# Background loads a tile ahead, background pieces between products, and the first up weights fetched during the output projection, in a fused retention, Fourier and convolutional FFN layer

## The chip, the core and the metric

The kernel runs as one program on one core of a Trainium2 chip. The metric is the device time of the whole program in microseconds. The five engines have in-order queues of their own: TensorE (PE) multiplies, VectorE (DVE), ScalarE (ACT) and GpSimd (POOL) compute elementwise, and SyncE (SP) issues most DMA transfers from one queue. Engines wait for each other by semaphores.

## What is computed

One layer of a diffusion backbone on 2048 tokens of width 1024, in float32. The part ahead of the change is a token mixer (retention heads and Fourier groups), followed by the parts that the change touches: the output projection with its norm and residual, and a gated convolutional FFN.

```python
x = x + gt_a * rms_norm(mix, g_mix_post)          # mix = concat(retention, fourier) @ w_out
h = modulate(rms_norm(x, g_ffn_pre), sh_f, sc_f)
u = conv3_along_rows(h @ w_up) + conv_b           # 1024 -> 2*2816, three taps within rows of 64 tokens
a, b = split(u)
x = x + gt_f * rms_norm((silu(a) * b) @ w_down, g_ffn_post)
```

## The kernel before

Tokens lie along the free axis, in four blocks `b` of 512; channels lie on the 128 partitions, in tiles `n` of 128 channels. Each float32 operand is split into a rounded half and a rest (`split`: ACT writes `hi`, DVE subtracts to get `lo`), and each product is made of three matmuls (`mm3`).

The stages follow one another on PE: context and value product; four retention heads; the Fourier part; the output projection; up pass 0 (token blocks 0 and 1); down pass 0; up pass 1 (blocks 2 and 3); down pass 1; a tail. The weights of the FFN are multiplied by a Strassen-like scheme with seven products instead of eight; the sums of weight blocks that it needs are made on the chip. Sums of the down weights (`wsum`) are made in `w_sums` while the retention heads run and are kept in device memory.

*Output projection.* `mix_mm` makes 32 products, block by block. Its square sums `accm` are reduced to one row by a matmul with ones (`mix_cols`: a `pc` product, then `rp` on DVE, then a power on POOL into `rcm`). `mix_rows` spreads the row over the partitions: for blocks 0 and 1 by a product (`pb`), for blocks 2 and 3 by a trip through device memory (`row_m`, `rr_m`). `mix_post` then scales a tile by the norm and the gate, adds the residual `xt`, stores the tile (`x`), and adds its squares to `accx`, which the second norm needs (`x2_cols`, `x2_rows`, `rr_n`). The list `steps` says after which product each of these pieces is written. Blocks 2 and 3 are left to `rest_of_mix`, a generator that runs in the background of up pass 0; their tiles (`mt`) come back from device memory.

*Up passes.* `up_pass` runs over weight tiles `j`. Those in `ones_` are single products; the others are pairs of seven products of 12 matmuls each (84 in a pair). `operands` loads the weights (`ur`, or in pass 1 stored sums `us`) and splits them into `u_a...` and `u_s...`, LEAD = 6 ahead of PE. In a pair the products `a`, `b`, `c`, `d` go to PSUM banks; `psf` (an add on DVE, line 1368) has to read bank `a` before the pair's seventh product, which `last_of_pair` writes in the middle of the next pair, can add to it. `conv` and `gate` (tiles `y`) follow on ACT, DVE and POOL, and stores of `y` go out by SP. After each pair, `run_some(bg, nbg)` runs `nbg` pieces of the background generators: 2 in pass 0, 3 (GN) in pass 1.

*Background of pass 1.* `Norm.squares` sums squares of the down product of pass 0, and `Norm.finish(True)` ends each of its two token blocks: column sums (`pc`, `rp`, `rcf`), a trip of the row through device memory (`row_f`, `rr_f`), then for each of eight tiles a load of the tile (`ft`) and of the residual (`xf`), a product and an add (on DVE for odd tiles, on POOL for even ones), and a store to `out`.

The order of the instructions on the engines is set by a list scheduler: each instruction has its place in the program as priority, and goes ahead of earlier ones whenever it is ready by the scheduler's own clock. `tc.high_priority` moves a stretch forward in that priority. So the place of a piece in the program is not its place in a queue.

Of the kernel before, what the change touches and what calls it, by code (L numbers as in the profile page):

```python
# [9 lines left out]
F32 = mybir.dt.float32  # L10
# [18 lines left out]
LATE_S = {"s1": "s3", "a12": "s4"}  # L29
# [11 lines left out]
FW = 2, 1, 3  # L41
# [8 lines left out]
SENG = {"s1": "vector", "s2": "vector", "s3": "vector", "s4": "vector"}  # L50
# [7 lines left out]
def kern(tc, A, out):  # L58
    nc = tc.nc

    with ExitStack() as es:
# [140 lines left out]
        def w_sums():  # L202

            for k in range(KH):
                for c in (slice(0, 256), slice(256, TB)):
                    w = sump.tile([P, 4, 256], F32, tag="sum", name="wsum")
                    for i in range(2):
                        nc.sync.dma_start(w[:, 2 * i:2 * i + 2], A["w_down"][k + KH * i].rearrange("p (n c) -> p n c", n=2)[:, :, c])
                    yield
                    for o, l, r, op in ((3, 1, 3, ALU.add), (1, 0, 1, ALU.subtract), (0, 3, 0, ALU.subtract), (2, 2, 0, ALU.subtract)):  # L210
                        nc.vector.tensor_tensor(w[:, o], w[:, l], w[:, r], op=op)
                        yield
                    nc.sync.dma_start(wds[k][:, :, c], w)
# [460 lines left out]
        ws = w_sums()  # L674
        units = []
# [89 lines left out]
        for part in range(2):  # L765
# [56 lines left out]
            for lt in range(4):  # L822
                p1, p3 = zprod(2 * part, lt), zprod(2 * part + 1, lt)
# [94 lines left out]
        tp, txt, trr, trm = tg(po_, "pt", 5), tg(po_, "xt", 3), tg(po_, "rr", 1), tg(po_, "rrm", 1)  # L918
# [16 lines left out]
        accm, accx, rcm, rrm, rrn, r2d = {}, {}, {}, {}, {}, {}  # L935

        def mix_post(b, n):
            if n == 0:
                accx[b] = po_.tile([P, TB], F32, tag="acc", name="accx", bufs=2)
# [6 lines left out]
            nc.sync.dma_start(xt, A["xT"][n, :, b * TB:(b + 1) * TB])  # L946
            nc.vector.scalar_tensor_tensor(m, m, G1[:, n:n + 1], rrm[b], ALU.mult, ALU.mult)
            nc.vector.tensor_tensor(m, m, xt, op=ALU.add)
            nc.sync.dma_start(x2scr[n][b], m)
            sq_add(tp, accx[b], m, n == 0)  # L950
# [42 lines left out]
        def mix_cols(b):  # L993
            rcm[b] = cst([P, 4], f"rcm{b}", po_)
            sum_cols(accm[b], rcm[b], 4, po_)

        def mix_rows(b):
            if b < 2:
                rrm[b] = bcast_row(trm, rcm[b], 4, f"m{b}")
            else:  # L1000
                rrm[b] = row_in(trm, row_out(rcm[b], 4, f"m{b}"), 4, f"m{b}")
# [111 lines left out]
        steps = {}  # L1113

        def at(t, f, *a):
            steps.setdefault(t, []).append((f, a))
        for b in range(NB - 1):
            for k in range(4):
                at(RS[0] * b + RS[1] * k // 2, load_r, b + 1, k)
        for b in range(NB):  # L1120
            at(8 * b + 9, mix_cols, b)
        at(10, mix_rows, 0)
        at(19, mix_rows, 1)
        T = {}
        tf = t_first(T, 0)
        for n in range(KT):
            at(11 + n, mix_post, 0, n)
            at(19 + n, mix_post, 1, n)
            at(24 + n, next, tf)
        at(20, x2_cols, 0)  # L1130
        at(22, x2_rows, 0)
        at(28, x2_cols, 1)
        for t in range(SEEDS):
            seed_mix(t)
        for t in range(32):
            mix_mm(t // KT, t % KT)
            for f, a in steps.get(t, ()):
                f(*a)


        def rest_of_mix():
            mix_cols(3)
            for b in (2, 3):
                mix_rows(b)
                yield
                for n in range(KT):
                    mix_post(b, n)
                    yield
# [610 lines left out]
```

## Time and profile before

| | |
|---|---|
| runs | 2265.41, 2267.44, 2261.84 us; median 2265.41 |
| profiled execution | 2262.55 us, of which the span is 2260.8 |
| granted TensorE clock, mean | 0.966 |
| PE busy | 2095.5 us, 93% of the span |
| DVE busy | 1608.3 us, 71% |
| ACT, POOL busy | 1009.6 us (45%), 678.4 us (30%) |
| data moved | 395.20 MB, 175 GB/s over the span |
| PE idle, released by `psf` on DVE | 57.0 us |
| PE idle, released by `u_a` on ACT | 16.5 us |

The stages in the profiled execution, in us from the start: context and value product to 190, heads to 600, Fourier part to 690, output projection to 837, up pass 0 to 1320, down pass 0 to 1541 (its end overlaps the first operands of up pass 1), up pass 1 to 2010, down pass 1 and tail to 2260.8. Busy time counts matmuls with modelled ends, so a stage in which PE is busy for all of its length has no gap, while a stage with gaps shows them as length less busy time. Idle time is put down to the engine whose semaphore ended it.

### The profile page before, as it was taken

Reading aid. Unit: us, or ns where it says so; the run is one execution under the profiler, and the core shown is the slowest. Engines: PE = TensorE matmul, PEld = TensorE weight load, DVE = VectorE, ACT = ScalarE, POOL = GpSimd, SP = SyncE. Lnnn points to the kernel's source line nnn. Section 1 sums busy time; section 2 is a strip of 40 time slices with the busy share of each in tenths; the row PEclk is TensorE's granted clock in tenths of the full one; section 3 lists DMA queues with packets and bytes.
Section 4 is the critical chain, followed back from the end, with each engine's and each line's share of the span. In section 5 each row is a group of like instructions: output and inputs, shape, how many; then the busy total and the mean of one; then the engine's idle time right before and its main releaser. Section 6 shows DMA issues by size and latency. Waiting matters only on the chain.

```text
span 2260.8 us, 28205 instructions
## 1 busy us (share of the span) xinstructions
PE 2095.5 (93%) x9819; PEld 1725.6 (76%) x9819; DVE 1608.3 (71%) x2301; ACT 1009.6 (45%) x1754; POOL 678.4 (30%) x541
## 2 busy tenths in 40 slices
PE   7999899999999977899999999998899799999996
PEld 3777778887888755678778888886678678888886
DVE  6887786767565469987888777778576566675557
ACT  4443233334444555445454544545345345553441
POOL 4102222222110553333433341133233322331016
PEclk9999999999999988999999999999999999999997
DMA  8676633325451363655645578655463554376553
GB/s 305 222 231 214 199 126 109 90 79 140 142 215 52 112 174 136 192 192 144 189 174 155 172 274 284 232 192 195 138 207 127 167 185 135 131 262 227 190 168 112
DMA packets 202590, 395.20 MB, mean 175 GB/s; under 512 B 31816, under 2 KB 69584, under 8 KB 202448
## 3 DMA queue, kind: packets, MB, share of 16 engines
q1 hardware_dynamic: 194416, 367.07, 50.1%
q0 software_dynamic: 7600, 26.23, 3.2%
q8 instruction: 77, 1.26, 0.2%
q14 instruction: 65, 0.53, 0.1%
q10 hardware_dynamic: 432, 0.11, 0.0%
HBM read 275.33 MB, written 118.00 MB: 174 GB/s over the span
## 4 chain that ended last, share of the span: by engine, by line
PE 37%; DVE 5%; DMA 4%; issue 2%; ACT 1%; POOL 1%; SPq 0%; DVEq 0%; ACTq 0%; POOLq 0%
PE psu L92 7%; PE psu L94 7%; PE psu L93 7%; PE psd L92 5%; PE psd L94 5%; PE psd L93 5%; DMA row_f<-rcf 1%; DMA xf<-x 1%; DVE y L1218 1%; DMA draw<-fb 0%; DMA ft<-fo 0%; DMA draw<-in_w_down 0%; DVE y L1219 0%; DVE u_a L85 0%; ACT y L1215 0%
## 5 line engine op out<-in xcount | busy, mean ns | idle before, releaser
L85 DVE TENSOR_TENSOR dlo<-draw,dhi 128x1024 fp32r<-128x1024 f32 x154 | 203.7, 1346 | 115.5 <-ACT dhi L84 101.7
L1259 POOL TENSOR_TENSOR y<-y,y 128x512 f32<-128x512 f32 x82 | 124.0, 1512 | 475.5 <-DVE y L1219 329.8
L93 PE MATMUL psd<-dlo,dhi 128*128 128x512 f32 (+1 forms) x660 | 248.7, 378 | 2.4 <-DVE dlo L85 2.4
L94 PE MATMUL psd<-dhi,dlo 128*128 128x512 f32 (+1 forms) x660 | 247.6, 377 | 0.0
L84 ACT CAST dhi<-draw 128x1024 fp32r<-128x1024 f32 x154 | 159.7, 1051 | 163.0 <-PE psd L94 112.7
L92 PE MATMUL psd<-dhi 128*128 128x512 f32 (+1 forms) x660 | 211.2, 378 | 0.6 <-DVE cx L1520 0.6
L92 PE MATMUL psu<-t,u_s 128*128 128x512 f32 x492 | 199.3, 405 | 7.3 <-ACT t L84 5.7
L93 PE MATMUL psu<-t,u_s 128*128 128x512 f32 x492 | 198.3, 403 | 4.5 <-DVE t L85 4.5
L94 PE MATMUL psu<-t,u_s 128*128 128x512 f32 x492 | 197.5, 401 | 0.0
L92 PE MATMUL psu<-b,u_a 128*128 128x512 f32 x424 | 168.2, 397 | 16.5 <-ACT u_a L84 16.5
L94 PE MATMUL psu<-b,u_a 128*128 128x512 f32 x424 | 166.9, 394 | 0.0
L93 PE MATMUL psu<-b,u_a 128*128 128x512 f32 x424 | 166.9, 394 | 0.0
L1215 ACT ACTIVATE y<-psu,cb,cw 128x512 f32<-128x512 f32 x135 | 104.6, 776 | 101.7 <-PE psu L94 74.8
L85 DVE TENSOR_TENSOR u_a<-ur,u_a 128x512 fp32r<-128x512 f32 x147 | 130.3, 890 | 23.5 <-ACT u_a L84 23.4
L93 PEld LDWEIGHTS psd<-dlo,dhi 128*128 128x128 f32 x660 | 126.0, 191 | 25.2 <-DVE dlo L85 2.8
L92 PEld LDWEIGHTS psd<-dhi 128*128 128x128 f32 x660 | 125.2, 191 | 23.3 <-DVE cx L1520 0.8
L94 PEld LDWEIGHTS psd<-dhi,dlo 128*128 128x128 f32 x660 | 125.9, 191 | 22.2
L1218 DVE SCALAR_TENSOR_TENSOR y<-psu,cw,y 128x504 f32<-128x504 f32 x135 | 99.5, 738 | 53.9 <-ACT y L1215 53.9
L85 DVE TENSOR_TENSOR u_s<-us,u_s 128x512 fp32r<-128x512 f32 x103 | 91.9, 893 | 46.7 <-ACT u_s L84 46.7
L92 PE MATMUL psu<-t,u_a 128*128 128x512 f32 x164 | 67.6, 412 | 57.0 <-DVE psf L1368 57.0
L92 PEld LDWEIGHTS psu<-t,u_s 128*128 128x128 f32 x492 | 97.0, 197 | 29.1 <-ACT t L84 7.3
L93 PEld LDWEIGHTS psu<-t,u_s 128*128 128x128 f32 x492 | 96.6, 196 | 27.6 <-DVE t L85 6.9
(435 smaller groups left out, 5393.7 us busy)
## 6 DMA issues: line engine op xcount, KB each, us to landing
ur<-in_w_up SPq DMA_DIRECT2D x74, 512.0 KB, 5.5
draw<-wd SPq DMA_DIRECT2D x88, 256.0 KB, 5.9
draw<-ft SPq DMA_DIRECT2D x88, 256.0 KB, 5.7
ft<-y SPq DMA_DIRECT2D x36, 512.0 KB, 6.1
draw<-in_w_down SPq DMA_DIRECT2D x66, 256.0 KB, 5.3
draw<-fb SPq DMA_DIRECT2D x66, 256.0 KB, 5.6
xt<-in_xT SPq DMA_DIRECT2D x56, 256.0 KB, 4.6
adaw<-in_wadaB SPq DMA_DIRECT2D x24, 512.0 KB, 6.5
```

Source lines behind the costliest of these rows:

```text
L84: nc.scalar.copy(hi, src)
L85: nc.vector.tensor_tensor(lo, src, hi.bitcast(F32), op=ALU.subtract)
L92: nc.tensor.matmul(ps, lhi, rhi, start=start, stop=False, skip_group_check=on)
L93: nc.tensor.matmul(ps, lhi, rlo, start=False, stop=False, skip_group_check=on)
L94: nc.tensor.matmul(ps, llo, rhi, start=False, stop=stop, skip_group_check=on)
L1215: nc.scalar.activation(y, ps, AF.Identity, bias=cb[:, j:j + 1], scale=cw[:, j, 1:2])
L1218: nc.vector.scalar_tensor_tensor(y3[:, :, 1:64], p3[:, :, 0:63], cw[:, j, 0:1], y3[:, :, 1:64], ALU.mult, ALU.add)
L1259: nc.gpsimd.tensor_tensor(y1, y1, y2, op=ALU.mult)
```

## The change

1. `w_sums` begins the load of the next `wsum` tile before it sums the current one.
2. `mix_post` is cut into `mix_load` (the loads) and the rest; `rest_of_mix` issues the loads of tile `n + 1` before it works on tile `n`, with one more empty piece after the row. The store of the norm's row (`row_out`) moves from `mix_rows` to `mix_cols`. The `accx` adds of blocks 0 and 1 go from POOL to DVE; those of blocks 2 and 3 stay on POOL.
3. `operands` issues its first load when it is made, and each next load before the weight sums and their stores; the splits lose their priority mark. The generator for pass 0 is made after product 26 of the output projection (`up0`), so its first two loads are written there. For pass 1, the first six operands are taken with `high_priority(offset=400)`.
4. Background pieces run inside a pair, one after each product named in `BGAT`: after products 1 and 4 in pass 0, after 0, 2 and 4 in pass 1. The number of pieces in a pair stays.
5. `Norm.finish(True)` loads a tile and its residual one tile ahead, behind the store of the last tile, and waits six pieces instead of three after the row's trip was issued.
6. In down pass 1 the last four squares of norm 0 are added on DVE. Pools: `xt` 4 tiles instead of 3, `rr` 2 instead of 1; the scratch of POOL's DMAs is 4096 instead of 8192 bytes. The first operands of block 0's page work (`tf`) are finished before `x2_rows(1)`.

```diff
-FW = 2, 1, 3
+FW = 2, 1, 6
+BGAT = (1, 4), (0, 2, 4)
...
         def w_sums():
...
+            nxt = begin()
+            while nxt:
+                w, (_, (a11, a12, a21, a22), dst) = nxt
+                nxt = begin() if todo else None
+                yield
...
-        tp, txt, trr, trm = tg(po_, "pt", 5), tg(po_, "xt", 3), tg(po_, "rr", 1), tg(po_, "rrm", 1)
+        tp, txt, trr, trm = tg(po_, "pt", 5), tg(po_, "xt", 4), tg(po_, "rr", 2), tg(po_, "rrm", 1)
...
+        def mix_post(b, n, loaded=None):
+            if n == 0:
+                accx[b] = po_.tile([P, TB], F32, tag="acc", name="accx", bufs=2)
+            m, xt = loaded or mix_load(b, n)
...
-            sq_add(tp, accx[b], m, n == 0)
+            sq_add(tp, accx[b], m, n == 0, nc.vector if b < 2 else nc.gpsimd)
...
+            def gen(nxt):
+                held = None
+                for i, (j, one) in enumerate(jobs):
+                    a = nxt
+                    if i + 1 < len(jobs):
+                        nxt = load(*jobs[i + 1])
...
+            return gen(load(*jobs[0]))
...
+        at(26, lambda: up0.append(up_load(0)))
...
+                got = mix_load(b, 0)
+                yield
                 yield
                 for n in range(KT):
-                    mix_post(b, n)
+                    now, got = got, mix_load(b, n + 1) if n + 1 < KT else None
+                    mix_post(b, n, now)
                     yield
...
                 def go(k, i, start):
...
                     next(extra, None)
+                    if i in BGAT[bb]:
+                        run_some(bg, 1)
...
                 pair(j, late_h() if j == twos[-1] else iter(()))
-                run_some(bg, nbg)
...
+                def fetch(n):
+                    f, xt = txt([P, TB], "ft"), txt([P, TB], "xf")
+                    nc.sync.dma_start(f, fos[self.b % 2][n // 2][:, n % 2])
+                    nc.sync.dma_start(xt, x2scr[n][self.b])
+                    return f, xt
+                got = fetch(0)
                 for n in range(KT):
...
+                    yield
+                    f, xt = got
+                    nc.vector.scalar_tensor_tensor(f, f, G2[:, n:n + 1], rr, ALU.mult, ALU.mult)
+                    (nc.vector if n % 2 else nc.gpsimd).tensor_tensor(f, f, xt, op=ALU.add)
+                    yield
+                    nc.sync.dma_start(out[n, :, self.t0:self.t0 + TB], f)
+                    if n + 1 < KT:
+                        got = fetch(n + 1)
...
-                begun.append(up_start(1))
+                begun.append(up_start(up_load(1), 400))
...
-                bg.append(norms[0].squares(range(4, 8)))
+                bg.append(norms[0].squares(range(4, 8), eng=nc.vector))
```

How the rows stand on the engines, at three places. First DVE at the end of the output projection, before: `rp` ends the column sums of a norm, `mt` are tiles of block 2 (scaled at L947, residual added at L948), `b_...` the `lo` halves of up operands from tokens, and `u_a` the first weights.

```order
L130 TENSOR_SCALAR rp<-pc 128x4
L947 SCALAR_TENSOR_TENSOR mt<-mt,G_5939,rr_m_7737 128x512 x2
L85 TENSOR_TENSOR b_2_7265<-m_0_6098,b_2_7265 128x512
L948 TENSOR_TENSOR mt<-mt,xt_7742 128x512
L85 TENSOR_TENSOR b_3_7287<-m_0_6153,b_3_7287 128x512
L85 TENSOR_TENSOR b_3_7309<-m_0_6153,b_3_7309 128x512
L1019 SCALAR_TENSOR_TENSOR h_7425<-m_1_5989,a_5941,rr_n_7317 128x512
L85 TENSOR_TENSOR u_a_7327<-ur_7319,u_a_7327 128x512
```

The same place on DVE after, where the `accx` adds are on this engine too:

```order
L129 TENSOR_SCALAR rp<-pc 128x4
L961 SCALAR_TENSOR_TENSOR mt<-mt,G_5939,rr_m_7667 128x512
L84 TENSOR_TENSOR b_2_7237<-m_0_6098,b_2_7237 128x512
L962 TENSOR_TENSOR mt<-mt,xt_7671 128x512
L961 SCALAR_TENSOR_TENSOR mt<-mt,G_5939,rr_m_7667 128x512
L962 TENSOR_TENSOR mt<-mt,xt_7798 128x512
L84 TENSOR_TENSOR b_2_7271<-m_0_6098,b_2_7271 128x512
L84 TENSOR_TENSOR b_3_7293<-m_0_6153,b_3_7293 128x512
L961 SCALAR_TENSOR_TENSOR mt<-mt,G_5939,rr_m_7667 128x512
L84 TENSOR_TENSOR u_a_7329<-ur_7188,u_a_7329 128x512
L962 TENSOR_TENSOR mt<-mt,xt_7883 128x512
L84 TENSOR_TENSOR b_3_7315<-m_0_6153,b_3_7315 128x512
```

The first `u_a` moved ahead of the last `b_3` and ahead of `h`; a third `mt` tile moved in front of it.

Second, DVE at the first norm finish of up pass 1, before, from the `rp` of its column sums on:

```order
L130 TENSOR_SCALAR rp<-pc 128x4
L85 TENSOR_TENSOR u_s_13144<-ur_12868,u_s_13144 128x512
L1218 SCALAR_TENSOR_TENSOR y_12987<-psf,cw,y_12987 128x8x63
L1219 SCALAR_TENSOR_TENSOR y_12987<-psf,cw,y_12987 128x8x63
L85 TENSOR_TENSOR u_a_13173<-ur_13010,u_a_13173 128x512
L1445 SCALAR_TENSOR_TENSOR ft<-ft,G_5943,rr_f_13139 128x512 x2
L85 TENSOR_TENSOR u_s_13193<-us,u_s_13193 128x512
```

And after:

```order
L129 TENSOR_SCALAR rp<-pc 128x4
L84 TENSOR_TENSOR u_a_13026<-ur_12866,u_a_13026 128x512
L84 TENSOR_TENSOR u_s_13047<-us,u_s_13047 128x512
L1480 SCALAR_TENSOR_TENSOR ft<-ft,G_5943,rr_f_13082 128x512
L84 TENSOR_TENSOR u_a_13062<-ur_12704,u_a_13062 128x512
L1246 SCALAR_TENSOR_TENSOR y_12864<-psu,cw,y_12864 128x8x63
L1480 SCALAR_TENSOR_TENSOR ft<-ft,G_5943,rr_f_13082 128x512
```

The first `ft` stands three rows behind `rp` instead of five, and the first two `ft` no longer follow each other.

Third, SP's queue in the same finish, before, with the loads of the up weights (`us`, `ur`) and the stores of `y` among the rows of the finish:

```order
L1441 DMA out<-ft 128x512
L1431 DMA ft<-fo_1_244 128x512
L1239 DMA fb_1_176<-y_12986 128x1024
L1165 DMA us<-wu_213 128x1024
L1436 DMA xf<-x_2_1_117 128x512
L1164 DMA ur_13314<-in_w_up 128x1024
L1166 DMA ur_13316<-wu_213 128x1024
L1441 DMA out<-ft 128x512
```

And after:

```order
L1483 DMA out<-ft 128x512 x2
L1473 DMA ft<-fo_1_244 128x512
L1474 DMA xf<-x_3_1_121 128x512
L1473 DMA ft<-fo_1_245 128x512
L1474 DMA xf<-x_4_1_125 128x512
L1483 DMA out<-ft 128x512
L1473 DMA ft<-fo_1_245 128x512
L1483 DMA out<-ft 128x512
L1474 DMA xf<-x_5_1_129 128x512
L1473 DMA ft<-fo_1_246 128x512
L1474 DMA xf<-x_6_1_133 128x512
L1483 DMA out<-ft 128x512
```

The finish's rows stand in one block, and the load of `wu_213` follows behind them (two rows below the last one shown, after one more `ft`).

More of the change, by code (lines that the diff above doesn't have):

```diff
@@ L933, in M, with mix_load @@
             return MP[b][n % 4][:, n // 4]
[L935 to L939, printed above, removed]
+        accm, accx, rcm, rrm, rrn, r2d, rowm = {}, {}, {}, {}, {}, {}, {}
+        def mix_load(b, n):
             if b < 2:
@@ L1566, in down_pass @@
             return C
+        for _ in tf:
+            pass
         x2_rows(1)
```

227 lines of the change are left out of this document (106 added, 121 removed).

## The prediction

> **What bounds the kernel now.** I read the page first, then a table of stages, then the waits and the single rows at the places that the change touches. The page says that TensorE is the bound, and which of its waits are largest:
>
> ```profile
> PE 2095.5 (93%) x9819; PEld 1725.6 (76%) x9819; DVE 1608.3 (71%) x2301; ACT 1009.6 (45%) x1754; POOL 678.4 (30%) x541
> ...
> L92 PE MATMUL psu<-b,u_a 128*128 128x512 f32 x424 | 168.2, 397 | 16.5 <-ACT u_a L84 16.5
> ...
> L92 PE MATMUL psu<-t,u_a 128*128 128x512 f32 x164 | 67.6, 412 | 57.0 <-DVE psf L1368 57.0
> ```
>
> PE is busy for 93% of the span. Its two large waits are for `psf` (57.0 us), an add on VectorE that frees a PSUM bank, and for `u_a` (16.5 us), the first weights of each up pass. The stages, with the length, then PE, PEld, DVE, ACT and POOL busy, and the granted clock:
>
> ```profile
> 690.00:845.00 155.00, 135.40 (x611) 111.36 (x609) 83.28 (x121) 86.20 (x165) 67.54 (x47) 0.94 0.41 116
> 845.00:905.00 60.00, 47.23 (x157) 34.69 (x158) 54.46 (x68) 33.09 (x57) 22.35 (x14) 0.78 0.43 152
> 905.00:1080.00 175.00, 160.75 (x690) 131.47 (x689) 145.74 (x188) 82.49 (x137) 62.96 (x41) 0.96 0.59 173
> 1080.00:1320.00 240.00, 229.41 (x1001) 187.49 (x1000) 200.66 (x262) 122.56 (x202) 90.51 (x61) 0.99 0.55 183
> 1320.00:1510.00 190.00, 190.00 (x840) 157.31 (x839) 137.36 (x140) 93.81 (x107) 46.37 (x49) 1.00 0.73 253
> 1510.00:1840.00 330.00, 289.43 (x1231) 236.88 (x1230) 218.23 (x285) 148.03 (x243) 107.37 (x77) 0.94 0.51 170
> ```
>
> Length less PE busy is what a stage can give: 19.6 us in the output projection (which here holds the start of up pass 0), 12.8 in the first pairs, 14.3 and 10.6 in the rest of up pass 0, nothing in down pass 0, where PE is busy without a gap, 40.6 in the start and first two thirds of up pass 1. Together 97.9 us. DVE is the nearly full engine of up pass 0: 145.74 of 175.
>
> **The projection and the first up loads.** Rows of PE, POOL, DVE, SP and ACT, each from the timeline (start, duration, and in brackets the idle time ahead and its releaser):
>
> ```profile
> 774.92 1.09 PE L162 MATMUL pc<-ones,accm 128*128 128x1 f32 x8 [1.80 <-POOL accm L157]
> ...
> 776.45 0.63 PE L93 MATMUL psmix<-rt,wr 128*128 128x512 f32 x1
> 776.88 0.63 PE L94 MATMUL psmix<-rt,wr 128*128 128x512 f32 x1
> ...
> 779.58 0.39 PE L92 MATMUL psmix<-rt,wr 128*128 128x512 f32 x1
> 779.81 0.39 PE L93 MATMUL psmix<-rt,wr 128*128 128x512 f32 x1
> ...
> 824.02 1.87 PE L162 MATMUL pc<-ones,accx 128*128 128x1 f32 x8 [4.22 <-POOL accx L157]
> ...
> 845.38 0.80 PE L92 MATMUL psu<-b,u_a 128*128 128x512 f32 x1 [8.13 <-ACT u_a L84]
> ```
> ```profile
> 822.26 1.71 POOL L157 TENSOR_TENSOR accx<-accx,sq 128x512 f32<-128x512 f32 x1
> ```
> ```profile
> 807.60 1.75 DVE L85 TENSOR_TENSOR b<-m,b 128x512 fp32r<-128x512 f32 x1
> ...
> 813.97 0.68 DVE L85 TENSOR_TENSOR b<-m,b 128x512 fp32r<-128x512 f32 x1
> ...
> 832.26 2.43 DVE L947 SCALAR_TENSOR_TENSOR mt<-mt,G,rr_m 128x512 f32<-128x512 f32 x2 [6.10 <-DMA x<-m]
> ```
> ```profile
> 836.77 0.45 SPq L1171 DMA_DIRECT2D ur<-in_w_up  x1
> ```
> ```profile
> 844.72 1.14 ACT L84 CAST u_a<-ur 128x512 fp32r<-128x512 f32 x2 [5.67 <-DMA ur<-in_w_up]
> ```
>
> Matmuls start 0.23 us apart at full clock (779.58, 779.81) and 0.43 apart after a gap (776.45, 776.88). A gap costs its idle time and some ten matmuls at 0.20 us more, so 2.0 us on top.
>
> The Trainium skill ("TensorE: Matmul & The Clock Gate", section "What's actually happening") says that the clock falls to half after at least one idle window of about 3.4 us. The trace does not bear that limit out here: the wait ahead of 774.92 was 1.80 us, and the half pace followed. By the page's rule the short gaps would cost no clock, and the term worked out next would be about 8 instead of 9.5.
>
> The squares' sums `accx` of token blocks 0 and 1 go from POOL to DVE: 16 adds at 1.71 us, 27 us, leave POOL, and 16 adds at 0.68 us (alone) to 1.75 (beside a POOL add) join DVE, 11 to 28 us. The wait at 824.02 ends with POOL's backlog, so with the move I expect 4 of its 4.22 + 2.0 us back; POOL's shorter line also brings the second `accm` in sooner, for which I take 2. The first weight loads are issued in the projection instead of at 836.77, so ACT's wait of 5.67 us goes. What is late next is DVE: its queue holds the `mt` behind the norm's row trip (832.26) in front of the last splits of the up operands, and in the new order three `mt` products with two adds and four splits stand between that and the first complete operand pair. Nine instructions at 0.68 to 1.2 us are some 8 us, so the first up product could start at 840.3, and the 6 us gained ahead of it move this to about 834 to 836. I take 836 against 845.4: **9.5 us**, of which 3.5 are the loads and 6 the sums. Bounds: loss of 3 (DVE's adds at 1.75 make the splits late) and gain of 20 (all 19.6 of the stage). The value stands nearer the middle because DVE's wait at 832.26 is untouched. The following pairs wait for operands that the same DVE queue makes, so they keep this gain and add none: 0, at most 12.8.
>
> **Up pass 0.** The waits of 905 to 1320 (total, times, longest), and one stretch of 40 us:
>
> ```profile
> PE psu L92 <- DVE psf L1368: 23.5, 8, 7.7
> ...
> DVE mt L948 <- DMA xt<-in_xT: 8.3, 7, 5.7
> ```
> ```profile
> 1080.00:1120.00 40.00, 36.46 (x155) 29.64 (x154) 37.06 (x48) 20.17 (x34) 13.11 (x9) 0.96 0.65 213
> ```
>
> The tile loaded ahead can remove DVE's 8.3 us of waiting for `xt`, and pieces between products spread the same DVE work within a pair. But the work itself stays, 21 to 29 DVE instructions from one `psf` to the next in the new order, as before, and DVE is busy for 37.06 of 40 us. What is late next is DVE itself. I take **6 us**: the 5.7 us wait and little else. Bounds: 0 and 30 (23.5 and three clock drops).
>
> **Up pass 1.** Waits of 1510 to 1840, and rows of one row trip of the second norm:
>
> ```profile
> PE psu L92 <- DVE psf L1368: 32.2, 5, 10.3
> ...
> DVE ft L1445 <- DMA ft<-fo: 22.9, 10, 6.3
> ...
> DVE ft L1445 <- DMA rr_f<-row_f: 20.2, 2, 10.3
> ...
> PE psu L92 <- ACT u_a L84: 8.4, 1, 8.4
> ```
> ```profile
> 1599.51 0.15 DVE L130 TENSOR_SCALAR rp<-pc 128x4 f32<-128x4 f32 x1
> ...
> 1614.93 1.42 DVE L1445 SCALAR_TENSOR_TENSOR ft<-ft,G,rr_f 128x512 f32<-128x512 f32 x2 [10.33 <-DMA rr_f<-row_f]
> ...
> 1630.56 0.69 DVE L1368 TENSOR_TENSOR psf<-psu,x 128x512 f32<-128x512 f32 x1
> ```
> ```profile
> 1601.18 0.37 SPq L135 DMA_DIRECT2D row_f<-rcf  x1
> ...
> 1611.88 0.32 SPq L140 DMA_DIRECT2D rr_f<-row_f  x1
> ```
> ```profile
> 1616.76 0.39 PE L92 MATMUL psu<-t,u_s 128*128 128x512 f32 x1
> ...
> 1620.62 0.39 PE L94 MATMUL psu<-b,u_a 128*128 128x512 f32 x1
> 1631.30 0.80 PE L92 MATMUL psu<-t,u_a 128*128 128x512 f32 x1 [10.30 <-DVE psf L1368]
> ```
> ```profile
> 1782.81 0.79 PE L92 MATMUL psu<-t,u_a 128*128 128x512 f32 x1 [7.85 <-DVE psf L1368]
> ```
>
> The start of the pass (8.4 and 2.0 of clock): DVE and ACT have their instructions there in the same order as before, and SP still has the first `ft` and now also `xf` ahead of the last weight draws. I cost it at 0, between a loss of 3 and a gain of 10.4.
>
> The norm's finish: `rp` at 1599.51 starts the row trip, DVE stands from about 1604 to 1614.93 at the first `ft`, and with everything behind it reaches `psf` at 1630.56, for which PE waits 10.30 us. The change says that six pieces, not three, come between the trip and the first `ft`. The new order does not keep them apart: `ft` stands three rows behind `rp`, where it stood five behind. The 20.2 us therefore stay. From `ft` to `psf` are 16 instructions where there were 17; at the old pace, 15.6 us over 17, that is 14.7. PE has 84 matmuls between the column sums and the product that waits, where it had 96: at 0.227 us from start to start (eighteen matmuls in a row, the first at 1616.76 and the last at 1620.62) 19.0 us instead of 21.8. So the gap becomes 10.30 - 0.9 + 2.8 = 12.2 us at the worst, and about 9.5 where the loads ahead save the short waits among those 15.6 us; I take 10.3, unchanged. In the second finish (7.85) the `psf` stands one row behind the first `ft`; PE has 48 matmuls, 10.9 us, against the trip of 15.4 (1614.93 less 1599.51), the `ft` and the `psf` of 1.42 and 0.69: 17.5, and some 7 us remain. The gain is in the tiles behind: three later `psf` waits make 32.2 - 10.3 - 7.85 = 14 us, with 5.4 for the clock 19.4, and `ft<-fo` waits of 22.9 us feed them. With loads a tile ahead I halve these. That is **9 us**, with bounds of a loss of 10 and a gain of 41.5 (32.2 and five clock drops).
>
> **Weight sums and the tail.** The first row is DVE's sums of weights from 60 to 300 us.
>
> ```profile
> L211 DVE TENSOR_TENSOR wsum<-wsum 128x256 f32<-128x256 f32 x88 | 38.5, 443 | 13.8 <-DMA wsum<-in_w_down 12.9
> ```
>
> A tile ahead takes 12.9 us of waiting from DVE there; DVE has other room, so I give it **3 us**, between 0 and 6. The last squares of the tail on DVE move four adds of 0.68 us to it and off POOL: 0, within 2.7 either way (four at 0.68). The smaller scratch for POOL's DMAs: nothing in the trace prices it; 0.
>
> **Sum.** 9.5 + 6 + 9 + 3 = 27.5 us off the profiled execution of 2262.55 (span 2260.8 and 1.75 around it) gives 2235.0. That execution lay 2.86 under the median of the runs, 2265.41, so I predict 2237.9, rounded **2238**.
>
> **Rivals.** Row trips hidden: if the pieces between products reach the chip as written and no `psf` waits for a norm, all 41.5 us of the finishes go instead of 9: 2238 - 32.5 = 2205. For it speaks that every other `ft` wait is a load; against it the order of DVE. Chance 0.16.
>
> DVE's load keeps everything but the projection: pass 0 and the finishes give 0, the sums too: 2238 + 18 = 2256. For it speaks 37.06 of 40; here the change, in effect, does not do what it says, since its pieces are put back beside the old neighbours. Chance 0.14.
>
> The moved sums give nothing: where every DVE add beside a POOL add takes 1.75 us, 16 take 28 us, and the 6 us of the sums are lost: 2244. The Trainium skill ("SBUF — State Buffer", section that describes the engine ports) says that a VectorE instruction with two SBUF inputs and a GpSimd one that reads SBUF lock each other out entirely. The rows 1.75 and 0.68 agree. Against it: with `accx` gone POOL has only half of its adds, so fewer meet. Chance 0.07.
>
> The weight loads of the up passes, from the page's DMA issues (count, size, us to landing):
>
> ```profile
> ur<-in_w_up SPq DMA_DIRECT2D x74, 512.0 KB, 5.5
> ```
>
> Slower: SP's one queue. In the new order thirteen entries of the finish, stores that wait for their add and fetches that stand behind the store, come in one block ahead of the next pair's weight loads. With 6.3 us for a fetch and 1.4 + 1.5 for the product and the add, a tile takes 9.2 us, and four in a row 37; PE has six operands in hand and one pair, 16.3 + 19.0 = 35.3 us. With 5.5 us for the load itself (the row above) the operands are late by 7 us, and 2.0 clock, in each of two finishes: 18, and no gain in them, 9, just eat the 27.5. At 12 us a tile (POOL's adds behind `y`) it is 18 + 2 each, 40 + 9: 2287. It decides from 9.2 us a tile on. Against it: some fetches go in pairs. Chance 0.09.
>
> **Chances.** The forecast has 0.54. A measurement of this kernel can't tell less than 0.3%, 6.8 us, from no change; 2256 is 0.4% under, so half of that rival counts as the same. Faster 0.54 + 0.16 + 0.07 + 0.07 = 0.84, same 0.07, slower 0.09. The range from 2200 to 2260 takes in 2205 and 2256.
>
> **What would show it.** In the new profile: `pc<-accx` without a wait of 4 us, the first `psu<-b,u_a` at about 836 with `u_a` waiting for DVE instead of a load; the `psf` total down from 57.0 to about 44, with two waits of 7 to 11 still there, each behind an `ft` that waits for `rr_f` about 10 us; `xt` gone from DVE's waits; SP without a wait that makes an `ur` late. I am wrong if the `rr_f` waits are covered, or if `us` or `u_s` appears among PE's waits.

## The result, and the profile after

| | before | after |
|---|---|---|
| median of 13 runs, us | 2264.93 (2261.28 to 2273.38) | 2251.50 (2244.14 to 2262.51) |
| profiled execution, us (span) | 2262.55 (2260.8) | 2252.89 (2251.1) |
| ratio of the runs | | 0.9942, 95% interval 0.9929 to 0.9955 |

The change makes the kernel 13.4 us faster, 0.6%. Forecast were 27.5 us and 2238; the measured median lies inside the range, at a little under half of the forecast gain. The two profiled executions are only 9.7 us apart; most of what they lack lies ahead of the output projection, as the second table shows.

The page of the changed kernel, its engines and the groups that answer to those of before:

```profile
PE 2096.0 (93%) x9819; PEld 1729.4 (77%) x9819; DVE 1621.3 (72%) x2322; ACT 1011.0 (45%) x1754; POOL 651.1 (29%) x520
...
L91 PE MATMUL psu<-b,u_a 128*128 128x512 f32 x424 | 167.5, 395 | 8.7 <-ACT u_a L83 8.7
L93 PE MATMUL psu<-b,u_a 128*128 128x512 f32 x424 | 166.7, 393 | 8.7 <-DVE u_a L84 8.7
...
L91 PE MATMUL psu<-t,u_a 128*128 128x512 f32 x164 | 68.0, 415 | 52.5 <-DVE psf L1397 52.5
```

The wait for `u_a` behind ACT has halved, but its second half has come back as a wait for `u_a` behind DVE, on the first product's third matmul instead of its first. The `psf` wait went from 57.0 to 52.5.

Where the time went is seen best by laying the two profiles beside each other at the same matmul. Each line is the time from one product to another in the timeline of PE (for pinned kernels, see the experiments):

| stretch, us | before | after | mt pinned | ft pinned | both pinned |
|---|---|---|---|---|---|
| start to first output projection product | 722.1 | 730.8 | 728.1 | 729.5 | 728.3 |
| output projection, first to last product | 113.9 | 104.5 | 102.9 | 103.2 | 102.9 |
| to the 85th matmul of up pass 0 | 31.1 | 30.6 | 24.8 | 32.1 | 23.9 |
| to the 1849th (its end) | 459.3 | 460.7 | 455.4 | 465.8 | 453.6 |
| to the 2017th (down pass 0, start of up pass 1) | 258.2 | 259.8 | 259.7 | 261.5 | 258.6 |
| to the 3697th (up pass 1) | 426.9 | 421.5 | 420.1 | 388.2 | 386.4 |
| to the end of the span | 249.4 | 243.4 | 242.5 | 243.7 | 244.1 |

The profiled execution with `ft` pinned (2225.79 us) was the slowest of its four runs, and lost its time in up pass 0, which the pin does not touch. So, between the profiles of before and after: 8.7 us lost ahead of the projection, 9.4 won in it, 0.5 at the first up products, 1.4 and 1.6 lost in pass 0 and around the down pass, 5.4 won in up pass 1, 6.0 behind it.

### The profile page after: what moved, and what is told of

The parts are those of the page before. It is cut to its first block, busy times and chain, and to the rows that moved or that the text cites. A ratio compares the mean times of both kernels' runs of the same rounds, so it can differ in the third digit from the quotient of the medians.

```text
span 2251.1 us, 28118 instructions
## 1 busy us (share of the span) xinstructions
PE 2096.0 (93%) x9819; PEld 1729.4 (77%) x9819; DVE 1621.3 (72%) x2322; ACT 1011.0 (45%) x1754; POOL 651.1 (29%) x520
## 4 chain that ended last, share of the span: by engine, by line
PE 60%; DVE 15%; DMA 11%; issue 6%; POOL 4%; ACT 3%; SPq 1%; DVEq 0%; POOLq 0%; ACTq 0%
PE psu L91 9%; PE psu L92 9%; PE psu L93 9%; PE psd L91 5%; PE psd L92 5%; PE psd L93 5%; DMA xf<-x 1%; DVE u_a L84 1%; PE pada L87 1%; DMA adaw<-in_wadaB 1%; DMA fr<-fscr 1%; DMA ur<-in_w_up 1%; DMA xt<-in_xT 1%; DVE u_s L84 1%; PE psk L93 1%
## 5 line engine op out<-in xcount | busy, mean ns | idle before, releaser
L84 DVE TENSOR_TENSOR u_a<-ur,u_a 128x512 fp32r<-128x512 f32 x147 | 142.2, 972 | 61.6 <-ACT u_a L83 61.4
L83 ACT CAST u_a<-ur 128x512 fp32r<-128x512 f32 x147 | 90.4, 621 | 123.6 <-PE psu L93 113.6
L92 PEld LDWEIGHTS psd<-dlo,dhi 128*128 128x128 f32 x660 | 124.9, 189 | 24.8 <-DVE dlo L84 2.6
L84 DVE TENSOR_TENSOR u_s<-us,u_s 128x512 fp32r<-128x512 f32 x103 | 92.8, 902 | 52.7 <-ACT u_s L83 52.5
L91 PEld LDWEIGHTS psu<-t,u_s 128*128 128x128 f32 x492 | 97.1, 197 | 29.7 <-ACT t L83 8.0
L91 PE MATMUL psu<-t,u_a 128*128 128x512 f32 x164 | 68.0, 415 | 52.5 <-DVE psf L1397 52.5
L92 PEld LDWEIGHTS psu<-t,u_s 128*128 128x128 f32 x492 | 97.1, 197 | 24.1 <-DVE t L84 3.2
L93 PEld LDWEIGHTS psu<-t,u_s 128*128 128x128 f32 x492 | 97.4, 198 | 21.2
```

The source lines that it names most:

```text
L83: nc.scalar.copy(hi, src)
L84: nc.vector.tensor_tensor(lo, src, hi.bitcast(F32), op=ALU.subtract)
L91: nc.tensor.matmul(ps, lhi, rhi, start=start, stop=False, skip_group_check=on)
L92: nc.tensor.matmul(ps, lhi, rlo, start=False, stop=False, skip_group_check=on)
L93: nc.tensor.matmul(ps, llo, rhi, start=False, stop=stop, skip_group_check=on)
```

## The experiments

All are the kernel before or the changed kernel with a few lines edited. "Pinned" means that an instruction is queued on DVE behind a named one; the scheduler may not put it ahead of that.

**ft pinned.** In up pass 1, the finish's products stay behind the last `psf` that the program has written ahead of them; the adds, which read what the products write, follow them.

```diff
-                nc.vector.tensor_tensor(ps["f"], ps["a"], x5, op=ALU.add)
+                LAST["psf"] = nc.vector.tensor_tensor(ps["f"], ps["a"], x5, op=ALU.add)
...
-                    nc.vector.scalar_tensor_tensor(f, f, G2[:, n:n + 1], rr, ALU.mult, ALU.mult)
+                    with tc.issue_after(LAST["psf"].ins):
+                        nc.vector.scalar_tensor_tensor(f, f, G2[:, n:n + 1], rr, ALU.mult, ALU.mult)
                     (nc.vector if n % 2 else nc.gpsimd).tensor_tensor(f, f, xt, op=ALU.add)
```

> The changed kernel with one thing added: in up pass 1 the DVE instructions of a norm's finish (ft products and adds) are queued behind the last psf that the program wrote ahead of them, so that they stand on DVE where the program has them, two pairs behind the row's trip. Theory A (the scheduler puts them forward to just behind rp, and DVE stands there for the row's trip with psf behind it): the waits of 9.6, 4.5, 8.4 and 4.1 us for psf in up pass 1 and the half clock after them go, together 36.5 us; the total falls to between 2215 and 2225. Theory B (DVE has too much work in these pairs, wherever the pieces stand): the psf waits only move to other pairs, and the total stays within 8 us of 2251.5.

Measured: 2218.15 us, ratio to before 0.9797 (0.9782 to 0.9811). Up pass 1 took 388.2 us instead of 421.5. What happened in the changed kernel without the pin, on DVE, and on PE behind it:

```profile
1583.66 0.15 DVE L129 TENSOR_SCALAR rp<-pc 128x4 f32<-128x4 f32 x1
...
1599.94 0.75 DVE L1480 SCALAR_TENSOR_TENSOR ft<-ft,G,rr_f 128x512 f32<-128x512 f32 x1 [11.33 <-DMA rr_f<-row_f]
...
1611.65 0.69 DVE L1397 TENSOR_TENSOR psf<-psu,x 128x512 f32<-128x512 f32 x1
```
```profile
1612.40 0.79 PE L91 MATMUL psu<-t,u_a 128*128 128x512 f32 x1 [9.62 <-DVE psf L1397]
```

DVE stands for 11.33 us at an `ft`, the next `psf` is behind it, and PE waits 9.62. With both pins (the kernel two experiments below), the same place on DVE and on SP:

```profile
1564.62 0.15 DVE L129 TENSOR_SCALAR rp<-pc 128x4 f32<-128x4 f32 x1
1581.63 0.69 DVE L1399 TENSOR_TENSOR psf<-psu,x 128x512 f32<-128x512 f32 x1
...
1601.56 0.69 DVE L1399 TENSOR_TENSOR psf<-psu,x 128x512 f32<-128x512 f32 x1
1602.75 0.75 DVE L1483 SCALAR_TENSOR_TENSOR ft<-ft,G,rr_f 128x512 f32<-128x512 f32 x1
```
```profile
1567.60 0.37 SPq L134 DMA_DIRECT2D row_f<-rcf  x1
1576.29 0.32 SPq L139 DMA_DIRECT2D rr_f<-row_f  x1
```

Between `rp` and the first `ft` lie 38 us and two `psf`, as the program has it with its six pieces; `rr_f` is issued 26 us ahead of the `ft`, and `ft` waits for nothing. Theory A holds: 33.4 us of medians, for the 36.5 that it added up.

**mt pinned.** The same for the tiles of blocks 2 and 3 in up pass 0; ahead of the first `psf`, behind the fourth weight operand.

```diff
-            nc.vector.scalar_tensor_tensor(m, m, G1[:, n:n + 1], rrm[b], ALU.mult, ALU.mult)
-            nc.vector.tensor_tensor(m, m, xt, op=ALU.add)
+            with tc.issue_after(LAST.get("psf", LASTU[3] if LASTU else None).ins) if b > 1 else nullcontext():
+                nc.vector.scalar_tensor_tensor(m, m, G1[:, n:n + 1], rrm[b], ALU.mult, ALU.mult)
+                nc.vector.tensor_tensor(m, m, xt, op=ALU.add)
...
-                split(w[:, 0], w[:, 1], a[nme])
+                LASTU.append(split(w[:, 0], w[:, 1], a[nme]))
```

> The changed kernel with the tiles of the output projection's rest (mt products and adds of blocks 2 and 3) queued on DVE behind the fourth up operand or the last psf that the program wrote ahead of them. Theory A (they are put forward; DVE waits in them for a row or a load while the first up operands and psf stand behind it): the wait of 8.7 us for u_a at the first up product goes to under 2, most of the psf waits in up pass 0 go (7.2, 2.8, 4.4, 4.0 and 3.2 with their half clock, together 31 us), and the total is between 2215 and 2230. Theory B (DVE is simply full in the first ten pairs, 146 of 175 us): the first product gains 8, the psf waits stay within 8 us of their sum, total 2238 to 2246.

Measured: 2234.36 us, 0.9870 (0.9858 to 0.9883), between the totals of the two theories, and the profile shows why. In the changed kernel DVE waits at the end of the projection, with PE behind it:

```profile
833.23 0.75 DVE L961 SCALAR_TENSOR_TENSOR mt<-mt,G,rr_m 128x512 f32<-128x512 f32 x1 [5.62 <-DMA rr_m<-row_m]
...
844.34 0.75 DVE L961 SCALAR_TENSOR_TENSOR mt<-mt,G,rr_m 128x512 f32<-128x512 f32 x1 [4.38 <-DMA mt<-x]
845.00 0.69 DVE L84 TENSOR_TENSOR u_a<-ur,u_a 128x512 fp32r<-128x512 f32 x1
```
```profile
845.75 0.80 PE L93 MATMUL psu<-b,u_a 128*128 128x512 f32 x1 [8.73 <-DVE u_a L84]
```

With the pin, the first product starts without a wait:

```profile
832.04 0.48 PE L91 MATMUL psu<-b,u_a 128*128 128x512 f32 x1
832.36 0.39 PE L92 MATMUL psu<-b,u_a 128*128 128x512 f32 x1
```

The stretch from the last projection product to the 85th matmul falls from 30.6 to 24.8. In the rest of up pass 0 the `psf` waits of 905 to 1320, changed kernel first, then with the pin, are

```profile
PE psu L91 <- DVE psf L1397: 23.6, 8, 7.2
```
```profile
PE psu L91 <- DVE psf L1399: 15.0, 9, 3.9
```

and the busy times of 905 to 1080, in the same order:

```profile
905.00:1080.00 175.00, 159.77 (x678) 129.98 (x677) 146.28 (x188) 81.05 (x136) 61.22 (x40) 0.95 0.54 180
```
```profile
905.00:1080.00 175.00, 167.70 (x731) 136.95 (x730) 160.74 (x203) 87.99 (x147) 68.08 (x43) 0.99 0.59 198
```

DVE does 161 us of work in 175 with the pin and 146 without, and PE 8 us more. So DVE was not full. Without the pin it stood 4.9 us for `xt` and 1.9 for `mt` in this stretch, with the pin for neither. A part was given back: from the 1093rd to the 1849th matmul the pinned kernel needs 182.1 us where the changed one needs 174.3, since pieces that had been done early now stand there, with three waits of 1.1 to 3.9.

**Both pinned.** Both edits on the changed kernel.

> The changed kernel with both pins: the ft products and adds of the spilled finish and the mt products and adds of blocks 2 and 3, each queued on DVE behind the last psf that the program wrote ahead of it (the first mt behind the fourth up operand). Theory A (each pin removes its own waits, in stages that do not overlap): 2251.5 - 33.4 - 17.1 = 2201, between 2196 and 2208. Theory B (time saved in pass 0 is given back at the start of up pass 1, whose first operands wait for DVE and SP): 2208 to 2216.

Measured: 2201.01 us, 0.9724 (0.9702 to 0.9745), 50 under the changed kernel: theory A, the two pins add up. It is the fastest version here. The stages 905 to 1080, 1080 to 1320 and 1510 to 1840, and all `psf` waits of PE:

```profile
905.00:1080.00 175.00, 167.89 (x732) 137.32 (x732) 161.05 (x203) 88.46 (x148) 69.49 (x44) 0.99 0.59 200
1080.00:1320.00 240.00, 230.95 (x1000) 188.31 (x999) 205.84 (x255) 122.61 (x197) 90.43 (x66) 0.99 0.57 197
1510.00:1840.00 330.00, 322.04 (x1421) 266.23 (x1420) 244.93 (x322) 172.64 (x283) 116.38 (x81) 0.99 0.58 184
```
```profile
PE psu L91 <- DVE psf L1399: 16.7, 11, 2.5
```

PE is busy 322 of 330 us in up pass 1 (289 before), and no `psf` wait is over 2.5 us.

**Both pins on the kernel before**, and nothing of the change. The `mt` edit is the one above; the finish's, for spilled tiles only:

```diff
                     if spilt or n in FV:
+                      with tc.issue_after(LAST["psf"].ins) if spilt else nullcontext():
                         t = nc.vector.scalar_tensor_tensor(f, f, G2[:, n:n + 1], rr, ALU.mult, ALU.mult)
...
+                    with tc.issue_after(LAST["psf"].ins) if spilt else nullcontext():
                         (nc.vector if spilt and n % 2 else nc.gpsimd).tensor_tensor(f, f, xt, op=ALU.add)
```

> The kernel before with both pins and nothing of the change: the ft products and adds of the spilled finish and the mt products and adds of blocks 2 and 3 are queued on DVE behind the last psf (the first mt behind the fourth up operand). Theory A (the places on DVE are what counts, and the loads have time enough in either kernel): up pass 1 loses its four waits behind the finishes and up pass 0 most of its own, and only what the changed projection brings is missing (the first up product still waits for its weights): 2264 - 33 - 9 = 2222, between 2215 and 2230. Theory B (without the loads a tile ahead, a piece that stands where the program has it waits there for its tile, in the middle of a pair, with psf behind it): psf waits of 30 us or more, total 2235 to 2255.

Measured: 2219.79 us, 0.9790 (0.9772 to 0.9807). Theory A: its `psf` waits are

```profile
PE psu L92 <- DVE psf L1370: 13.5, 10, 3.1
```

Up pass 1 takes 387.0 us here as against 386.4 with the change, so there the loads a tile ahead are worth nothing that the profiles show once the pieces stand where they should. The change is worth 18.8 us between the two pinned kernels (2219.8 and 2201.0): 10.6 in the projection (113.5 to 102.9), 4.8 at the first up products (28.7 to 23.9), 5.9 behind up pass 1 (250.0 to 244.1). In up pass 0 the pinned kernel before is not slower either, 452.8 against 453.6.

**accx on DVE alone.**

```diff
-            sq_add(tp, accx[b], m, n == 0)
+            sq_add(tp, accx[b], m, n == 0, nc.vector if b < 2 else nc.gpsimd)
```

> The kernel before with one part: the accx adds of token blocks 0 and 1 on DVE instead of POOL. Theory A (POOL's backlog is what the pc products of the projection wait for, and the 9.4 us that the projection gained come from this part alone): the projection takes 104 to 107 us from its first to its last product instead of 113.9, but the first up product still waits for its weights, so that about half of it is lost there; total 2255 to 2260. Theory B (a DVE add beside a POOL add takes as long as POOL's, so the wait only changes its engine): projection 112 to 116, total within 3 us of 2264.

Measured: 2261.86 us, 0.9994 (0.9978 to 1.0010): no change. The projection does shrink, to 102.3 us (first product 724.5, last 826.8), more than theory A asked. But the first up product takes all of it back, and not half:

```profile
847.97 0.80 PE L92 MATMUL psu<-b,u_a 128*128 128x512 f32 x1 [16.05 <-ACT u_a L84]
```
```profile
845.50 0.69 DVE L948 TENSOR_TENSOR mt<-mt,xt 128x512 f32<-128x512 f32 x1 [13.19 <-DMA xt<-in_xT]
```

The first weights are issued 3.5 us earlier than before (833.23 and 836.77) and their split on ACT starts 2.6 us later (847.30 and 844.72), and DVE waits 13.19 us for one `xt`. Theory A is right on the mechanism and wrong on the total, theory B the other way round.

**Pieces after the pair again**, on the changed kernel.

```diff
-                    if i in BGAT[bb]:
-                        run_some(bg, 1)
...
                 pair(j, late_h() if j == twos[-1] else iter(()))
+                run_some(bg, nbg)
```

> The changed kernel with the background pieces written after each pair again (2 in pass 0, 3 in pass 1) instead of inside it; all else as changed. Theory A (the scheduler places the pieces by their readiness, wherever the program writes them): total within 5 us of 2251.5 and the psf waits within 6 us of 52.5. Theory B (the places inside the pair are what brought the gain in up pass 1): the 4 us of up pass 1 are lost, total 2255 to 2260, and psf waits of 57 or more.

Measured: 2257.09 us, 0.9972 (0.9954 to 0.9990), `psf` waits of 62.4:

```profile
L91 PE MATMUL psu<-t,u_a 128*128 128x512 f32 x164 | 67.9, 414 | 62.4 <-DVE psf L1395 62.4
```

Theory B in size, but not in place: the pieces inside the pair are worth some 5.6 us of medians. In the profile up pass 1 takes 422.8 us here and 421.5 with the change, so little of it is lost there, and up pass 0 takes 469.1 (460.7 with the change, but 465.8 with `ft` pinned, whose order there is that of the change). The intervals of the two kernels' ratios to before, 0.9954 to 0.9990 and 0.9929 to 0.9955, just touch.

**The old w_sums**, in the changed kernel.

```diff
-            nxt = begin()
-            while nxt:
-                w, (_, (a11, a12, a21, a22), dst) = nxt
-                nxt = begin() if todo else None
+            for k in range(KH):
+                for c in (slice(0, 256), slice(256, TB)):
+                    w = sump.tile([P, 4, 256], F32, tag="sum", name="wsum")
```

> The changed kernel with the former w_sums (one tile loaded, summed, stored). In it, the order of the instructions up to the middle of the output projection is that of the kernel before. Theory A (the second wsum tile, begun early, moves DMA and DVE work against the context and value products and the heads, and costs them 8.7 us): the output projection starts at about 722 us from the start of the span, as before, instead of 730.8, and the total falls from 2251.5 to about 2243. Theory B (those 8.7 us are the scatter from one execution to the next): it starts anywhere from 722 to 731 and the total stays within 3 us of 2251.5.

Measured: 2254.13 us, 0.9958 (0.9943 to 0.9973), projection from 730.5. Theory B: the start lies between 722 and 731 and the total within 3 us. The late start is not from `w_sums`, for it is there without it. The loads a `wsum` tile ahead changed nothing that these runs can tell (2251.5 against 2254.1, with intervals that overlap).

**The smaller scratch**, on the kernel before.

```diff
-    nc = _bacc.Bacc("TRN2", target_bir_lowering=False, num_devices=1, dynamic_dma_scratch_size=8192)
+    nc = _bacc.Bacc("TRN2", target_bir_lowering=False, num_devices=1, dynamic_dma_scratch_size=4096)
```

> The kernel before with the scratch of POOL's DMAs at 4096 instead of 8192 bytes, and nothing else; the order of all instructions is that of before. In the profiles so far the output projection starts at 722.1 and 722.7 us where the scratch is 8192 (before, and before with the new tail) and between 728.1 and 730.8 in the four kernels where it is 4096. Theory A (the smaller scratch, or the addresses that move with it, costs this): start at 728 to 731, total 2270 to 2273. Theory B (the other pool sizes of the change, which only the four have, or their later work): start at 722 to 723, total within 3 us of before.

Measured: 2263.86 us, 0.9998 (0.9986 to 1.0010), projection from 727.8 us. The total is theory B's, the start nearly theory A's. With the old `w_sums`, six profiled kernels have the order of before up to the projection: before (722.1), the new tail (722.7), `accx` (724.5), both pins on before (726.2), the scratch (727.8), and the changed kernel with the old `w_sums` (730.5). One and the same order takes 722 to 730 us. The first four of them, which have the pools and the scratch of before too, differ by 4.1 us, so at least that much is scatter of single executions. Whether the scratch and the pool sizes of the change cost a few us of the 8.7 is open: the five profiled kernels with the new `w_sums` start at 725.7 to 730.8.

**The tail alone**, on the kernel before: the last squares of norm 0 on DVE, and the adds of norm 1's odd tiles too.

```diff
-                    (nc.vector if spilt and n % 2 else nc.gpsimd).tensor_tensor(f, f, xt, op=ALU.add)
+                    (nc.vector if n % 2 else nc.gpsimd).tensor_tensor(f, f, xt, op=ALU.add)
...
-                bg.append(norms[0].squares(range(4, 8)))
+                bg.append(norms[0].squares(range(4, 8), eng=nc.vector))
```

> The kernel before with the tail's part of the change alone: the last four squares of norm 0 and the adds of the odd tiles of norm 1's finish on DVE instead of POOL. Theory A (POOL's queue was what the last column sums waited for): the two column sums at the end come 6 to 8 us earlier, total 2257 to 2259 against 2265. Theory B (what the changed kernel gained behind its last down products came from work that was already done earlier): within 3 us of 2265. Up to the last products of down pass 1 the order is that of before, so this run's profile also shows how much the start of the output projection at 722 us differs from one execution to the next.

Measured: 2262.03 us, 0.9990 (0.9979 to 1.0001). By the total this is theory B. The profile shows a gain, short of theory A's 6 to 8 us: from the 3697th up matmul to the end 244.7 us (2010.9 to 2255.6), where before has 249.4 and the change 243.4. The medians show 1.7, with up to 4.8 in the interval. The eleven profiled kernels agree with a gain of this size: the four with the old tail need 247.4 to 250.0 us for this stretch, the seven with the new one 242.5 to 244.7. It lies between the two column sums at the end, before:

```profile
2229.77 0.88 PE L162 MATMUL pc<-ones,accf 128*128 128x1 f32 x4 [2.62 <-DVE accf L157]
...
2246.95 0.98 PE L162 MATMUL pc<-ones,accf 128*128 128x1 f32 x4 [2.72 <-DVE accf L1663]
```
```profile
2236.00 3.01 DVE L1641 TENSOR_TENSOR cx<-cx,xf 128x256 f32<-128x256 f32 x1
...
2241.78 0.41 DVE L1641 TENSOR_TENSOR cu<-cu,xf 128x256 f32<-128x256 f32 x1
```

and the same column sums in the changed kernel:

```profile
2225.12 0.58 PE L161 MATMUL pc<-ones,accf 128*128 128x1 f32 x4 [2.11 <-DVE accf L156]
...
2238.14 0.58 PE L161 MATMUL pc<-ones,accf 128*128 128x1 f32 x4 [1.65 <-DVE accf L1690]
```

Between them lie 17.2 us before and 13.0 with the change, and 13.0 in this kernel (2229.07 to 2242.09). Before, POOL still adds tiles of the finish at 2233.85 and 2236.30, and an add of DVE takes 3.01 us there, where another takes 0.41. Which of the two moves brings the gain was not tried.

## Why the prediction was half right

The change was faster, as forecast, and gained a little under half of what was forecast. In the pair of profiles the terms are 9.9 for a forecast 9.5 (projection and first loads), a loss of 1.4 for 6 (up pass 0), 5.4 for 9 (up pass 1), 6.0 for 0 (tail), a loss of 1.6 around the down pass, and 8.7 lost ahead of the projection, where a gain of 3 had been forecast (weight sums). The step that failed most is up pass 0: I took DVE's wait for a load as a gain of PE, and then took DVE for full because it was busy for 37 of 40 us. What the runs showed instead is that tiles stand on DVE ahead of their place in the program, with `psf` behind them; putting them back is worth 17.1 us (`mt`, up pass 0 and the first up products) and 33.4 us (`ft`, up pass 1) on top of the change.

*Projection and first loads, 9.5 us:* 9.9 in the profile (9.4 and 0.5), the right size, but split otherwise than I had it, and partly by luck. I gave 6 to the sums and 3.5 to the loads. The sums brought 9.4, and the loads next to nothing, because of what I had named as late next: DVE at the `mt` behind the norm's row trip. Counted from the first projection product, which came 8.7 us later in the new profile, I had the first up product at 113.9 us; its first matmul started at 105.5, and its third, behind `u_a` on DVE, at 114.9. Two errors in my count met there. The first `mt` behind the row trip came 7.7 us sooner (102.4 where it had been 110.1), not 6, and I had left out the second wait, 4.38 us for a tile that the third `mt` loads (844.34). That `mt` stands in the rows of the change, ahead of the first `u_a`; I counted it as an instruction and did not ask when its load would land. Nor are there 16 adds to move: 14 leave POOL (541 instructions before, 527 with `accx` alone), since the first square of each block is no add. Alone, the sums are worth 0 (2261.9), so they need the loads; the loads alone were not run. With `mt` pinned the first up products gain 5.8 us more, so DVE's order limited both.

*Up pass 0, 6 us:* a loss of 1.4. The step that failed is the price, "the 5.7 us wait and little else". DVE's wait of 5.69 us for that `xt` was worth 3.54 to PE before:

```profile
1080.37 1.75 DVE L948 TENSOR_TENSOR mt<-mt,xt 128x512 f32<-128x512 f32 x1 [5.69 <-DMA xt<-in_xT]
```
```profile
1088.98 0.50 PE L92 MATMUL psu<-t,u_a 128*128 128x512 f32 x1 [3.54 <-DVE psf L1368]
```

It went, but DVE still waited 4.9 us for `xt` in the changed kernel, and its largest such wait stands ahead of PE's largest:

```profile
932.27 0.69 DVE L962 TENSOR_TENSOR mt<-mt,xt 128x512 f32<-128x512 f32 x1 [3.79 <-DMA xt<-in_xT]
```
```profile
935.48 0.80 PE L91 MATMUL psu<-t,u_a 128*128 128x512 f32 x1 [7.18 <-DVE psf L1397]
```

The `psf` waits of 905 to 1320 are 23.6 us, as against 23.5. The loss is hardly an accident of one execution: up pass 0 takes 457.5 to 459.3 us in the four profiled kernels that have nothing of the change there (before, `accx`, scratch, tail) and 460.7 to 465.8 in the three that have all of it unpinned (changed, `ft` pinned, old `w_sums`). The other step that failed is "what is late next is DVE itself". DVE's 37 of 40 us looked like a full engine, and the change kept the work; the pins showed that the same work, done where the program has it, leaves PE 8 us more in 175, with DVE busier. I took a busy share for a limit where the order of a queue was one.

*Up pass 1, 9 us:* 5.4. The two row trips stayed, as forecast: 9.62 for a forecast 10.3, 8.36 for 7. The three later waits, which I halved, were two of 4.46 and 4.08 us, where there had been 5.06, 5.71 and 3.26. That is 14.0 down to 8.5, 5.5 us where I had taken 7 off; the rest of the 9, which I had counted for the clock, does not show in the 5.4 of this stretch. DVE's waits for `ft<-fo` fell from 22.9 to 6.3 us, but what is left still stands ahead of both of these `psf`: DVE waited 3.9 us for tiles ahead of the first and, in these rows, 4.4 ahead of the second:

```profile
1792.53 0.75 DVE L1480 SCALAR_TENSOR_TENSOR ft<-ft,G,rr_f 128x512 f32<-128x512 f32 x1 [1.35 <-DMA ft<-fo]
...
1796.14 0.69 DVE L1481 TENSOR_TENSOR ft<-ft,xf 128x512 f32<-128x512 f32 x1 [1.60 <-DMA xf<-x]
...
1801.34 1.45 DVE L1480 SCALAR_TENSOR_TENSOR ft<-ft,G,rr_f 128x512 f32<-128x512 f32 x1 [1.49 <-DMA ft<-fo]
```

DVE's waits for the row trips are 20.2 us before and 21.1 after:

```profile
PE psu L91 <- DVE psf L1397: 27.0, 5, 9.6
...
DVE ft L1480 <- DMA rr_f<-row_f: 21.1, 2, 11.3
...
DVE ft L1480 <- DMA ft<-fo: 6.3, 5, 2.3
```

*Start of up pass 1, 0:* right, 8.4 us before and 8.7 after.

*Weight sums, 3 us, and tail, 0:* the first was not seen. DVE's waits for the `wsum` loads, 12.9 us before, did not go but were 18.1:

```profile
L221 DVE TENSOR_TENSOR wsum<-wsum 128x256 f32<-128x256 f32 x88 | 43.9, 508 | 18.7 <-DMA wsum<-in_w_down 18.1
```

The tail gave 6.0 in the profile, outside the 2.7 that I had allowed, and I had passed over one of its edits: the finish's adds of odd tiles had been on DVE for spilled tiles only, and are there for the last finish as well. Seven instructions leave POOL (541 to 534 with the tail alone), not four.

*Rivals:* that every row trip would be hidden, for 32.5 us more than the forecast, did not happen with the change; that is what the `ft` pin does, alone, and it is worth 33.4 us over the change. The rival of moved sums that give nothing falls by the projection's 9.4 us. Its mechanism is there, in two `accx` adds of the changed kernel, the first while POOL adds (`accm`, 797.4 to 803.6 us) and the second while it does not:

```profile
800.68 1.79 DVE L156 TENSOR_TENSOR accx<-accx,sq 128x512 f32<-128x512 f32 x1
...
806.07 0.68 DVE L156 TENSOR_TENSOR accx<-accx,sq 128x512 f32<-128x512 f32 x1
```

The Trainium skill ("SBUF — State Buffer", section "SBUF: two separate sides") has the two engines lock each other out for a whole instruction, and these rows agree. Enough of the adds did not meet one of POOL's.

The one queue of SP: at the place named, thirteen rows in a block, the block took from 1607.8 to 1626.6 us, and PE then waited for `psf` (4.46 us at 1638.16), not for operands, so that it decided nothing. The nearest to what happened was the rival that the pieces are put back beside their old neighbours. Half of its mechanism holds: the pieces are put back, but it is their order on DVE and not DVE's load that keeps the gain. Its sum, 2256, is 4.5 over the median.

## What to carry to other kernels

Where a scheduler orders the queues by its own clock, a piece that is written later in the program need not stand later on its engine: look at the row that waits longest, find where the program has it, and if the two differ, pin it there before anything else is tuned. An engine that is busy 90% is not shown to be full while its queue holds a wait for a load; moving the waiting instruction tests it. Two parts that shorten two waits in a row are to be costed together, since the wait that ends last keeps the gain of the other.

## What was not expected of the hardware

A load can take far longer than its median. An `xt` of 256 KB that lands in 4.5 us in the median of the kernel with `accx` alone kept DVE there for 13.19 us at the end of the projection. The stores of the projection's last tiles, the loads of `mt` and `xt`, and the first up weights were issued within 11 us around it (824 to 835); that this burst is what delayed it was not tested.

The first 722 to 730 us of the kernel, with the same order on every engine, differ by 8 us between profiled executions, 4.1 of them with the same pools and scratch. Much of it is gathered early: the adds of `wsum` run from 63.0 to 294.1 us in the fastest of these and from 62.3 to 300.1 in the slowest. So a pair of profiles alone does not tell a difference of less than that in the whole. The changed kernel may lose some time there for good. It is 18.3 us ahead of the kernel before from the projection on, in the profiles, and 13.4 in the medians; the gap of 4.9 is close to the 4.6 by which the mean start of the five kernels with the new `w_sums` (728.5) lies behind that of the four with the pools of before (723.9); no run settles it.

Half pace of the matmuls follows some short waits of PE and not others. In the changed kernel a wait of 2.76 us (960.04) is followed 1.3 us later by seven matmuls 0.42 to 0.43 us apart; before, a wait of 3.22 us (1132.20) is followed by matmuls 0.22 to 0.24 apart throughout. So the 2.0 us that I put on top of a gap is not the price of every gap.
